# Turning the stored states' rows with VectorE and a scratch instead of TensorE, with the skip term of the stream tokens ahead and the decay moved

## The chip, the cores and the metric

The kernel runs on one core of a Trainium2 chip. Its engines are TensorE (PE in the profile; PEld is its weight load), VectorE (DVE), ScalarE (ACT), GpSimd (POOL) and SyncE (SP). Each works through its own queue in order; semaphores tie the queues together. SP, ACT and POOL issue DMAs. The metric is device microseconds for one execution; less is better. Before the change the median of three runs is 2634.31 us (2633.36 to 2634.69).

## What is computed

One layer of a hybrid encoder, for 256 tokens of a new stream (prompt) and 8 running streams of 16 tokens each, 384 tokens in all. The part that matters here is the state-space branch: per head h, the output of a token t is what the tokens before it in its chunk give, what the stored state gives, and a skip term.

```python
y = jnp.einsum('btsgr,bsgrp->btgrp', cb[..., None] * decay, xdt)
y = y + jnp.einsum('btgn,bgrpn->btgrp', Cc, h) * jnp.exp(cum)[..., None]
h = h * jnp.exp(last)[..., None, None] + jnp.einsum('bsgn,bsgr,bsgrp->bgrpn', Bc, w_end, xdt)
...
y = y + d_skip[..., None] * xh
a_ssd = gated_rmsnorm(y.reshape(b, L, D_INNER), z, ssd_norm)
```

The prompt starts from a zero state, so the second line matters only for the 128 tokens of the running streams. All is float32; the large products split each operand into a rounded high part and the rest (three products each).

## The kernel before

Activations lie with channels on partitions and the 384 tokens along the free axis: 256 prompt tokens, then 128 stream tokens. Most of the time goes into projections: `proj` multiplies 128 output channels' weights with all tokens, in two halves of eight weight tiles. A half's weights come by a DMA on SP (`wfetch`, L63) into one of three buffers and are split by ACT (`wh_...`, L70) and DVE (`wl_...`, L71), each into one of three buffers, so that a split is at most two halves ahead of TensorE. A half takes TensorE 3.9 us (24 products, whose starts are 0.163 us apart).

The state-space stage is a loop over 8 groups g. In each, ten projections run on TensorE: four heads' pairs of channels as tiles x0 to x3, the group's B and C, and four gate tiles z0 to z3. A convolution (`conv_in`, `taps`) follows each x, B and C tile on DVE and ACT. `turned` turns x and B tiles token-major: a DVE transpose of 32x32 blocks, four DMAs on POOL's queue into a scratch `t_scr` that move the blocks to their place, and reads from it.

The four channel tiles of a group make two pairs, `D.p[0]` and `D.p[1]` (four heads each). TensorE does the small products of a pair in one uninterrupted block between projections. The block of pair 0 stands behind z3 of its own group, that of pair 1 behind x2 of the next. It has these parts, by line of the profile:

- `t_pp` (L750): the prompt's new state. In pair 1's block `t_cb` (L695) follows, C times B.
- `t_yT` (L717): two 128x128 transposes of `yis`, the stored state's part of y, scaled by the decay and token-major, to channel-major in the columns 256 to 383 of the PSUM tiles `Y` (one for each of the two channel tiles).
- `t_Y` (L736): 24 products of 64x64 tiles, the part within the chunks, into `Y` and `Yb`. For the stream tokens they add to what the transposes left.
- `t_yi` (L704): C times the stored state `hs`, for the next pair; `yside` (DVE, L790) scales it into `yis`.
- `state` (L865): four tiles `su`, which DVE adds to `hs` (L874).

`Y`, `Yb`, `su` and the norm's `bc_g` come from one pool of six PSUM buffers, `cb` too. Behind the block, `final` on DVE adds skip term and `Y` for all 384 tokens (L889), then `Yb` (L900), and multiplies with z (L901).

`dside` (L856) multiplies the loaded state with its decay, 128x2048 elements in one DVE instruction, after `t_yi` has read it and before `state` adds to it. For pair 0 it stands in the program ahead of z1; `fside` (L850) masks the pair's decay matrix E; `finish` and `store` norm the group before, with a chain of small DVE instructions (L187 to L191). The rest of `pd`'s tiles are SBUF tiles of this stage.

The order on each queue is not the program's order: a scheduler places the instructions, and `behind(...)`, `later()` (behind the latest weight split of ACT and DVE) and `dve_later()` hold some of them back. Behind the stage, during the last eight gate projections (`gate_b`), `aload` reads the branch's 32 normed tiles back from `a_scr` through SP (L1094) and splits them (L1098, L1099).

Of the kernel before, what the change touches and what calls it, by code (L numbers as in the profile page):

```python
# [14 lines left out]
P = 128  # L15
# [6 lines left out]
G = 8  # L22
# [11 lines left out]
def build(ctx, tc, io):  # L34
# [18 lines left out]
    def sstile(name):  # L53
        return pss.tile([P, 512], F32, tag="ss", name=name)
# [19 lines left out]
    def dve_later():  # L74
        return behind(cut[1])
# [138 lines left out]
    ma_scr = [dram.tile([P, T], F32, name=f"ma_scr{i}") for i in range(KD)]  # L214
    gb_scr = [dram.tile([P, T], F32, name=f"gb_scr{i}") for i in range(KD)]
    t_scr = [dram.tile([T, P], F32, name=f"t_scr{i}") for i in range(40)]
    d_scr = dram.tile([P, NH], F32, name="d_scr")
    cum_scr = dram.tile([NH, T], F32, name="cum_scr")
    dec_scr = dram.tile([NH, NB], F32, name="dec_scr")
# [363 lines left out]
    with tc.tile_pool(name="phd", bufs=2, reuse_waits="tile") as pd, tc.tile_pool(  # L583
# [126 lines left out]
                    )  # L710
            return i

        def t_yT(S):
            S.Ys = []
            for q in range(2):
                Y = sstile(f"Y{S.nm}_{q}")
                i = te.transpose(Y[:, TP:T], S.yis[:, q], ident)  # L717
                S.Ys.append(Y)
            S.Yb = sstile(f"Yb{S.nm}")
            return i  # L720

        lower, upper = slice(0, 64), slice(64, P)

        def t_Y(S):
            for q in range(2):
                Ya, Yb = S.Ys[q], S.Yb[:, q * TP : q * TP + TP]
                for r, sb, e0, n, o, c0 in (
                    (lower, 0, 0, TP, Ya, 0),
                    (upper, 0, 64, 192, Yb, 0),
                    (upper, 1, TP, P, Yb, 64),  # L730
                    (lower, 1, TP + 64, 64, Ya, 192),
                    (lower, 2, T + 64, 64, Ya, TP + 64),
                    (upper, 2, T, 64, Yb, 192),
                ):
                    for h in range(2):
                        i = te.matmul(  # L736
                            o[h * 64 : h * 64 + 64, c0 : c0 + n],
                            S.xdt[r, q, sb, h * 64 : h * 64 + 64],
                            S.E[r, q * 2 + h, e0 : e0 + n],
                            start=r is upper and q + sb == 0,  # L740
                            stop=sb > 0,
                            skip_group_check=True,
                        )
            return i
# [43 lines left out]
        def yside(S):  # L788
            S.yis = pd.tile([P, 2, P], F32, tag="yis", name=f"yis{S.nm}", bufs=1)
            S.ready = v.tensor_tensor(  # L790
                S.yis.rearrange("p j (h q) -> p (j h) q", h=2),
                S.yi.rearrange("p (h q) -> p h q", h=4),
                tok[:, 10, S.h0 : S.h0 + 4].unsqueeze(2).to_broadcast([P, 4, 64]),
                ALU.mult,
            )

        def xside(S):
            S.xdt = pd.tile([P, 2, 3, P], F32, tag="xdt", name=f"xdt{S.nm}", bufs=1)
# [59 lines left out]
        def state(S):  # L858
# [18 lines left out]
            lump(t_su)  # L877
            gp.dma_start(io["new_ssm_s"][S.qd], S.hs)

        def final(S):  # L880
            D, g = S.D, S.g
            pe = pd.tile([P, 2, P], F32, tag="pe", name=f"pe{S.nm}", bufs=1)
            s.copy(pe, even_odd(S.pp))
            s.dma_start(io["new_ssm_p"][S.qd], pe.rearrange("p j n -> p (j n)"))
            if S.jp == 0:
                D.ssum = pd.tile([P, T], F32, tag="ssum", name=f"ssum{g}", bufs=1)
            for q, j in enumerate(S.js):
                x, z = D.xs[j], D.zs[j]
                i = v.scalar_tensor_tensor(  # L889
                    out=x,  # L890
                    in0=x,
                    scalar=vec[:, V_DSK + g * 4 + j : V_DSK + g * 4 + j + 1],
                    in1=S.Ys[q][:, :T],
                    op0=ALU.mult,
                    op1=ALU.add,
                )
# [41 lines left out]
        for g in range(G + 1):  # L938
            if g == G:
                S = prev.p[1]  # L940
                work = [
                    [lambda: xside(S)],
                    [lambda: hside(S), lambda: eside(S, 0)],
                    [],
                    [lambda: eside(S, 1)],
                    [lambda: dside(S)],
                    [lambda: expside(S)],
                    [lambda: fside(S, 0), lambda: fside(S, 1)],
                    [],
                ]  # L950
# [9 lines left out]
                lump(lambda: t_yT(prev.p[1]))  # L960
# [46 lines left out]
            if g:  # L1007
                dside(prev.p[1])
                fside(prev.p[1], 0)
            D.CT = conv(u0 + 3, 40 + g, "CT", 2)  # L1010
            D.done = silu[0]
            if g:
                fside(prev.p[1], 1)
            cside(D)
            b2 = conv_in(u0 + 4, g * 4 + 2)
            S = D.p[0]
# [2 lines left out]
                lump(lambda: t_pp(prev.p[1], S.py))  # L1019
            lump(lambda: t_cb(D))  # L1020
            if g:
                lump(lambda: t_yT(prev.p[1]))
                lump(lambda: t_Y(prev.p[1]))
            lump(lambda: t_yi(S))
            mside(D)
# [1 line left out]
            if g:  # L1027
                state(prev.p[1])
                final(prev.p[1])
            D.xs.append(taps(b2, g * 4 + 2, "xs", 6))  # L1030
            with nullcontext() if g else behind(S.ready):
                xside(S)
# [42 lines left out]
            final(S)  # L1075
            if g:
                with behind(S.taken):
                    store(prev)
# [515 lines left out]
```

## Time and profile before

| | us |
|---|---|
| median of three runs | 2634.31 |
| the profiled execution's own time | 2633.2 |
| its span, first to last instruction | 2631.4 |
| TensorE busy in the span | 2621.3 |
| DVE busy in the span | 1573.0 |
| one group of the state-space stage (985.00 to 1072.70) | 87.70 |

The span is what the trace covers. A row of the timeline gives the start from the span's beginning, the length, engine, line, operation, what it writes and reads, the size and, in brackets, how long the engine was idle before and what ended that. A row of the grouped views gives count, busy time and the mean of one in ns. Granted clock is 0.999 of full speed.

### The profile page before, as it was taken

The page shows a single profiled execution, that of the slowest core. Times are in us where ns is not written, and L with a number is a line of the kernel's source. Part 1 is how long each engine was busy: PE and PEld are TensorE (multiplying, and loading weights), DVE is VectorE, ACT ScalarE, POOL GpSimd, SP SyncE. Part 2 cuts the span into 40 slices and gives each one's busy share as a digit, 9 for nine tenths or more (in the row PEclk, how much of TensorE's full clock was granted, in tenths as well). Part 3 has the DMA queues.
Part 4 walks back from the last instruction along what each step waited for, and adds up shares of the span by engine and source line. Part 5 has one row for each costly group of instructions (what it writes and reads, how often), then busy time and mean ns, then how long its engine had stood idle before and what let it go on. Part 6 is the DMA issues. An engine that isn't in the chain of part 4 may idle for free.

```text
span 2631.4 us, 40780 instructions
## 1 busy us (share of the span) xinstructions
PE 2621.3 (100%) x16189; PEld 2523.4 (96%) x16189; DVE 1573.0 (60%) x2286; ACT 1159.7 (44%) x1789; POOL 368.6 (14%) x545
## 2 busy tenths in 40 slices
PE   9999999999999999999999999999999999999998
PEld 9999999999999999999999989999999999989897
DVE  6685335799999999967444436434444444444446
ACT  6443324657565756555333336433333333333233
POOL 0000003245444444411000000000000000000000
PEclk9999999999999999999999999999999999999999
DMA  7445446667676767757545544444444444444443
GB/s 276 150 133 156 148 147 223 201 210 238 224 239 211 235 228 238 233 188 260 165 160 160 195 149 133 144 136 136 134 134 135 136 136 136 136 136 136 135 135 131
DMA packets 134256, 456.33 MB, mean 173 GB/s; under 512 B 20545, under 2 KB 27521, under 8 KB 129073
## 3 DMA queue, kind: packets, MB, share of 16 engines
q1 hardware_dynamic: 103552, 361.44, 43.0%
q0 software_dynamic: 23456, 77.47, 8.5%
q10 hardware_dynamic: 7056, 14.81, 1.8%
q8 instruction: 127, 2.08, 0.3%
q14 instruction: 65, 0.52, 0.1%
HBM read 409.27 MB, written 44.37 MB: 172 GB/s over the span
## 4 chain that ended last, share of the span: by engine, by line
PE 99%; DMA 0%; DVE 0%; ACT 0%; SPq 0%; issue 0%; DVEq 0%
PE pj_up L101 6%; PE pj_up L103 6%; PE pj_up L102 6%; PE wd L156 6%; PE wd L155 6%; PE wd L154 6%; PE pj_x L101 5%; PE pj_x L102 5%; PE pj_x L103 5%; PE pj_sp L102 3%; PE pj_z L103 3%; PE pj_z L102 3%; PE pj_z L101 3%; PE pj_sp L103 3%; PE pj_sp L101 3%; PE pj_gb L101 2%
## 5 line engine op out<-in xcount | busy, mean ns | idle before, releaser
L101 PE MATMUL pj_up<-x1h,wh_up 128*128 128x384 f32 (+1 forms) x1024 | 333.7, 326 | 0.0
L103 PE MATMUL pj_up<-x1h,wl_up 128*128 128x384 f32 (+1 forms) x1024 | 333.4, 326 | 0.0
L102 PE MATMUL pj_up<-x1l,wh_up 128*128 128x384 f32 (+1 forms) x1024 | 333.4, 326 | 0.0
L71 DVE TENSOR_TENSOR wl_wd<-w_wd,wh_wd 128x1024 fp32r<-128x1024 f32 x126 | 154.4, 1225 | 240.3 <-ACT wh_wd L70 240.3
L154 PE MATMUL wd<-wh_wd,hh 128*128 128x512 f32 x756 | 286.5, 379 | 0.0
L155 PE MATMUL wd<-wl_wd,hh 128*128 128x512 f32 x756 | 286.5, 379 | 0.0
L156 PE MATMUL wd<-wh_wd,hl 128*128 128x512 f32 x756 | 286.5, 379 | 0.0
L70 ACT ACTIVATE wh_wd<-w_wd 128x1024 fp32r<-128x1024 f32 x126 | 133.1, 1057 | 321.5 <-PE wd L156 261.0
L70 ACT ACTIVATE wh_up<-w_up 128x1024 fp32r<-128x1024 f32 x126 | 133.1, 1057 | 291.9 <-PE pj_up L102 231.7
L71 DVE TENSOR_TENSOR wl_up<-w_up,wh_up 128x1024 fp32r<-128x1024 f32 x126 | 154.4, 1225 | 178.1 <-ACT wh_up L70 178.0
L101 PE MATMUL pj_x<-xgh,wh_x 128*128 128x384 f32 x768 | 251.9, 328 | 0.0
L102 PE MATMUL pj_x<-xgl,wh_x 128*128 128x384 f32 x768 | 250.4, 326 | 0.0
L103 PE MATMUL pj_x<-xgh,wl_x 128*128 128x384 f32 x768 | 250.4, 326 | 0.0
L102 PEld LDWEIGHTS pj_up<-x1l,wh_up 128*128 128x128 f32 x1024 | 193.6, 189 | 0.2
L101 PEld LDWEIGHTS pj_up<-x1h,wh_up 128*128 128x128 f32 x1024 | 193.6, 189 | 0.2
L103 PEld LDWEIGHTS pj_up<-x1h,wl_up 128*128 128x128 f32 x1024 | 193.6, 189 | 0.0
L101 PE MATMUL pj_z<-xgh,wh_z 128*128 128x384 f32 x512 | 166.9, 326 | 0.0
L102 PE MATMUL pj_z<-xgl,wh_z 128*128 128x384 f32 x512 | 166.9, 326 | 0.0
L103 PE MATMUL pj_z<-xgh,wl_z 128*128 128x384 f32 x512 | 166.9, 326 | 0.0
L101 PE MATMUL pj_sp<-abh,wh_sp 128*128 128x384 f32 x512 | 166.9, 326 | 0.0
L102 PE MATMUL pj_sp<-abl,wh_sp 128*128 128x384 f32 x512 | 166.9, 326 | 0.0
L103 PE MATMUL pj_sp<-abh,wl_sp 128*128 128x384 f32 x512 | 166.9, 326 | 0.0
(351 smaller groups left out, 6373.6 us busy)
## 6 DMA issues: line engine op xcount, KB each, us to landing
w_up<-w_up SPq DMA_DIRECT2D x128, 512.0 KB, 3.5
w_wd<-w_down SPq DMA_DIRECT2D x128, 512.0 KB, 3.5
w_x<-w_in SPq DMA_DIRECT2D x96, 512.0 KB, 3.9
w_z<-w_in SPq DMA_DIRECT2D x64, 512.0 KB, 4.4
w_sp<-w_ssd SPq DMA_DIRECT2D x64, 512.0 KB, 3.5
w_ga<-w_ga SPq DMA_DIRECT2D x32, 512.0 KB, 3.6
w_pp<-w_pp SPq DMA_DIRECT2D x32, 512.0 KB, 3.4
hs<-ssm POOLq DMA_DIRECT2D x16, 1024.0 KB, 6.3
```

The source lines that it names most:

```text
L70: cut[0] = s.activation(h, w, AF.Copy)
L71: cut[1] = v.tensor_tensor(l, w, h.bitcast(F32), ALU.subtract)
L101: te.matmul(out, wh, xh, start=first, stop=False, **how)
L102: te.matmul(out, wh, xl, start=False, stop=False, **how)
L103: return te.matmul(out, wl, xh, start=False, stop=last, **how)
L154: te.matmul(out, mh, vh, start=k == 0 and b != held, stop=False, skip_group_check=b == held)
L155: te.matmul(out, mh, vl, start=False, stop=False, skip_group_check=b == held)
L156: last[0] = te.matmul(out, ml, vh, start=False, stop=k == nk - 1, skip_group_check=b == held)
```

## The change

The transposes `t_yT` go. In their place `yspread` lets DVE transpose the 32x32 blocks of `yis` right after `yside` (128x256), and four DMAs on POOL's queue write them to a new scratch `y_scr`, where they lie channel-major. `yfetch` reads them back into an SBUF tile `yT` with a DMA on ACT's queue, some three projections later. `preside` (two DVE instructions of 128x128) then forms skip term plus `yT` for the stream tokens in x itself, ahead of the block. `final` adds `Y` in two instructions in place of one: skip term and `Y` for the 256 prompt tokens, and `Y` alone for the second half of the stream tokens (64 columns; the first half lies in `Yb`). In `t_Y` the first product into `Y` now starts the accumulation. For pair 0, `dside` moves from ahead of z1 to behind z2 and `preside`.

```diff
+    y_scr = [dram.tile([TP, P], F32, name=f"y_scr{i}") for i in range(2 * G)]
...
-        def t_yT(S):
-            S.Ys = []
-            for q in range(2):
-                Y = sstile(f"Y{S.nm}_{q}")
-                i = te.transpose(Y[:, TP:T], S.yis[:, q], ident)
-                S.Ys.append(Y)
+        def t_Y(S):
+            S.Ys = [sstile(f"Y{S.nm}_{q}") for q in range(2)]
             S.Yb = sstile(f"Yb{S.nm}")
...
-                            start=r is upper and q + sb == 0,
+                            start=sb == 0 and (r is lower or q == 0),
...
+        def yspread(S):
+            S.yb = pd.tile([P, TP], F32, tag="yb", name=f"yb{S.nm}", bufs=1)
+            v.transpose(S.yb, S.yis.rearrange("p j n -> p (j n)"))
+            scr = y_scr[S.qd]
+            for q in range(4):
+                p32 = slice(q * 32, q * 32 + 32)
+                gp.dma_start(
+                    scr[:, p32].rearrange("(j a) b -> a j b", a=32), S.yb[p32].rearrange("p (j b) -> p j b", b=32)
+                )
+
+        def yfetch(S):
+            S.yT = pd.tile([P, 2, P], F32, tag="yT", name=f"yT{S.nm}", bufs=1)
+            with later():
+                s.dma_start(S.yT, y_scr[S.qd].rearrange("(q p) t -> p q t", q=2))
...
+        def preside(S):
+            for q, j in enumerate(S.js):
+                x = S.D.xs[j][:, TP:]
+                with dve_later():
+                    v.scalar_tensor_tensor(
+                        out=x, in0=x, scalar=dskip(S.g, j), in1=S.yT[:, q], op0=ALU.mult, op1=ALU.add
+                    )
...
-                i = v.scalar_tensor_tensor(
-                    out=x,
-                    in0=x,
-                    scalar=vec[:, V_DSK + g * 4 + j : V_DSK + g * 4 + j + 1],
-                    in1=S.Ys[q][:, :T],
-                    op0=ALU.mult,
-                    op1=ALU.add,
-                )
+                xp, xl = x[:, :TP], x[:, TP + 64 :]
+                Y = S.Ys[q]
+                i = v.scalar_tensor_tensor(out=xp, in0=xp, scalar=dskip(g, j), in1=Y[:, :TP], op0=ALU.mult, op1=ALU.add)
+                v.tensor_tensor(xl, xl, Y[:, TP + 64 : T], ALU.add)
...
             with nullcontext() if g else behind(S.split):
                 bside(D)
-            dside(S)
+            yfetch(S)
             zproj(1)
...
             fside(S, 1)
             zproj(2)
+            preside(S)
+            dside(S)
             zproj(3)
             S1 = D.p[1]
             S1.py = mmtile(f"py{S1.nm}")
             lump(lambda: t_pp(S, S1.py))
-            lump(lambda: t_yT(S))
             lump(lambda: t_Y(S))
             lump(lambda: t_yi(S1))
             yside(S1)
             state(S)
             final(S)
+            yspread(S1)
```

For pair 1, `yspread` stands behind `final` of the pair before, `yfetch` ahead of the next group's C tile and `preside` behind `fside`; the last group's pair 1 has the same calls among the gate projections.

What the scheduler makes of it on DVE's queue, group 6, pair 0. Before, the decay (`hs<-hs,decb`) stands between the splits of B and the weights of z2:

```order
L766 TENSOR_TENSOR Bhl_11045<-Bt_10489,Bhl_11045 128x256
L768 SCALAR_TENSOR_TENSOR Bd_11046<-BD_10490,vec,Bd_11046 128x256
L856 TENSOR_TENSOR hs_0_10592<-hs_0_10592,decb 128x2048
L71 TENSOR_TENSOR wl_z_2_0_11056<-w_z_2_0_11053,wh_z_2_0_11055 128x1024
L71 TENSOR_TENSOR wl_z_2_1_11090<-w_z_2_1_11087,wh_z_2_1_11089 128x1024
L850 TENSOR_TENSOR E_0_10944<-E_0_10944,cbm_10802 128x1024 x2
```

The weights of z2 are the next thing that TensorE needs from it. After the change the decay and the two skip terms (`xs<-xs,vec,yT`) stand here, between the weights of z3 and the first read of `Y` by `final`:

```order
L896 SCALAR_TENSOR_TENSOR xs_10521<-xs_10521,vec,yT_0_11193 128x128
L189 TENSOR_TENSOR na_g_11272<-ny_g_11273 128x384
L896 SCALAR_TENSOR_TENSOR xs_10722<-xs_10722,vec,yT_0_11193 128x128
L190 TENSOR_TENSOR na_g_11272<-na_g_11272,ssum_10423 128x384
L865 TENSOR_TENSOR hs_0_10724<-hs_0_10724,decb 128x2048
L191 SCALAR_TENSOR_TENSOR ny_g_11273<-na_g_11272,ny_g_11273 128x384
L1062 TENSOR_TENSOR zs_2_11349<-pj_z_2_11288,rstd 128x384
L71 TENSOR_TENSOR wl_x_0_11359<-w_x_0_11356,wh_x_0_11358 128x1024
L71 TENSOR_TENSOR wl_x_1_11389<-w_x_1_11386,wh_x_1_11388 128x1024
L1062 TENSOR_TENSOR zs_3_11416<-pj_z_3_11355,rstd 128x384
L71 TENSOR_TENSOR wl_x_0_11522<-w_x_0_11519,wh_x_0_11521 128x1024
L911 SCALAR_TENSOR_TENSOR xs_10521<-xs_10521,vec,Y_0_0_11426 128x256
```

So three instructions have come in ahead of the read of `Y`, two of them new, and none has left that stretch. On SP's queue, at the end of the last group, the first four reads of `a_scr` (`ar`) stood between the weights of z3 before:

```order
L63 DMA w_z_3_0_12194<-w_in 128x1024
L1094 DMA ar_13114<-a_scr_72 128x384
L1094 DMA ar_13120<-a_scr_73 128x384
L1094 DMA ar_13156<-a_scr_74 128x384
L1094 DMA ar_13162<-a_scr_75 128x384
L63 DMA w_z_3_1_12224<-w_in 128x1024
```

Now the same four stand among the weights of the last gate projections:

```order
L63 DMA w_gb_1_13480<-w_gb 128x1024
L1114 DMA ar_13290<-a_scr_72 128x384
L1114 DMA ar_13296<-a_scr_73 128x384
L1114 DMA ar_13332<-a_scr_74 128x384
L1114 DMA ar_13338<-a_scr_75 128x384
L63 DMA w_gb_0_13527<-w_gb 128x1024
```

They have moved behind 25 weight loads (the last of z3 and 24 of the gate), and the other 28 follow them in a changed mix with the weights.

More of the change, by code (lines that the diff above doesn't have):

```diff
@@ L711, in t_yi @@
             return i
-        def t_yT(S):
-            S.Ys = []
-            for q in range(2):
-                Y = sstile(f"Y{S.nm}_{q}")
-                i = te.transpose(Y[:, TP:T], S.yis[:, q], ident)
-                S.Ys.append(Y)
-            S.Yb = sstile(f"Yb{S.nm}")
-            return i
         lower, upper = slice(0, 64), slice(64, P)
         def t_Y(S):
+            S.Ys = [sstile(f"Y{S.nm}_{q}") for q in range(2)]
+            S.Yb = sstile(f"Yb{S.nm}")
             for q in range(2):
@@ L878, in state, with dskip @@
             gp.dma_start(io["new_ssm_s"][S.qd], S.hs)
+        def dskip(g, j):
+            return vec[:, V_DSK + g * 4 + j : V_DSK + g * 4 + j + 1]
+        def preside(S):
[5 more added lines that the diff above has]
+                    )
         def final(S):
@@ L944, in build @@
                     [],
-                    [lambda: eside(S, 1)],
+                    [lambda: eside(S, 1), lambda: yfetch(S)],
                     [lambda: dside(S)],
                     [lambda: expside(S)],
-                    [lambda: fside(S, 0), lambda: fside(S, 1)],
+                    [lambda: fside(S, 0), lambda: fside(S, 1), lambda: preside(S)],
                     [],
@@ L959, in build @@
                 py = mmtile("pp_last")
-                lump(lambda: t_yT(prev.p[1]))
                 lump(lambda: t_Y(prev.p[1]))
@@ L1009, in build @@
                 fside(prev.p[1], 0)
+            if g:
+                yfetch(prev.p[1])
             D.CT = conv(u0 + 3, 40 + g, "CT", 2)
@@ L1013, in build @@
                 fside(prev.p[1], 1)
+                preside(prev.p[1])
             cside(D)
@@ L1021, in build @@
             if g:
-                lump(lambda: t_yT(prev.p[1]))
                 lump(lambda: t_Y(prev.p[1]))
@@ L1029, in build @@
                 final(prev.p[1])
+            yspread(S)
             D.xs.append(taps(b2, g * 4 + 2, "xs", 6))
```

## The prediction

> **What bounds the kernel now.** I read the share of busy time and the chain that ended last first.
>
> ```profile
> PE 2621.3 (100%) x16189; PEld 2523.4 (96%) x16189; DVE 1573.0 (60%) x2286; ACT 1159.7 (44%) x1789; POOL 368.6 (14%) x545
> PE 99%; DMA 0%; DVE 0%; ACT 0%; SPq 0%; issue 0%; DVEq 0%
> ```
>
> TensorE is busy for 2621.3 of 2631.4 us, and the chain runs through it alone. Work taken from it is gained in full, as long as nobody makes it wait. So the second view is the stage that the change touches, over one group (one period of the loop over g; columns: PE, PEld, DVE, ACT, POOL busy with counts, clock, DMA share, GB/s).
>
> ```profile
> 985.00:1072.70 87.70, 87.70 (x672) 85.76 (x672) 80.07 (x124) 56.11 (x106) 41.09 (x56) 1.00 0.69 229
> ```
>
> DVE, 60% busy on the page, is 91% busy here (80.07 of 87.70 us). TensorE does not wait in this group, but DVE is close enough that the moment at which each of its results comes decides. The third view is therefore the timeline, TensorE first, at the block of pair 0 of group 6 (columns: start, length, engine, line, operation, count).
>
> ```profile
> 1024.88 0.83 PE L750 MATMUL py<-xhl,Bhl 128*128 128x256 f32 x6
> 1025.55 0.38 PE L717 MATMUL Y<-cst,yis 128*128 128x128 f32 x2
> 1025.86 0.43 PE L736 MATMUL Y<-E,xdt 64*64 64x256 f32 x2
> ...
> 1028.36 0.72 PE L865 MATMUL su<-xd,Bd 32*128 32x256 f32 x16
> ```
>
> The four su tiles and the three Y tiles of a pair share six PSUM buffers, so the fourth su tile takes the buffer of the pair's first Y and cannot start before DVE has read it (L889). Against that, DVE's timeline just before:
>
> ```profile
> 1005.93 2.29 DVE L856 TENSOR_TENSOR hs<-hs,decb 128x2048 f32<-128x2048 f32 x1
> 1008.13 2.35 DVE L71 TENSOR_TENSOR wl_z<-w_z,wh_z 128x1024 fp32r<-128x1024 f32 x2
> ...
> 1025.08 0.56 DVE L1044 TENSOR_TENSOR zs<-pj_z,rstd 128x384 f32<-128x384 f32 x1 [0.99 <-PE pj_z L103]
> 1026.07 1.23 DVE L71 TENSOR_TENSOR wl_x<-w_x,wh_x 128x1024 fp32r<-128x1024 f32 x1 [0.43 <-ACT wh_x L70]
> 1027.21 0.61 DVE L889 SCALAR_TENSOR_TENSOR xs<-xs,vec,Y 128x384 f32<-128x384 f32 x1
> ```
>
> L889 ends at 1027.82, su begins at 1028.36: a margin of 0.54 us, with 1.42 us (0.99 + 0.43) of DVE idle time ahead of it.
>
> **The transposes removed.** Their own row, and what they take of the path:
>
> ```profile
> L717 PE MATMUL Y<-cst,yis x32: 272/273/273, 499.6 to 1148.1; 128*128 128x128 f32 x32
> ```
>
> Two of them stand in each of 16 blocks. From the first one's start to the next product 0.31 us pass (1025.55 to 1025.86). The two together last 0.38 and one 0.273, so the second starts 0.11 after the first; the other 0.20 is one more 0.11 and some 0.09 of the passage from whole-array work to 64*64 tiles, which a product that now follows L750 directly will pay too. Gain per block 0.22 us, at most 0.31; over 16 blocks 3.5 us, at most 5.0. I take 3.5, because the passage stays. The start flag moves from the transpose to the first Y product and adds no instruction: nothing, unless a started accumulation is slower, of which no row says anything.
>
> The Trainium skill, "VectorE: DVE Perf Modes", section "Rules for kernel authors", speaks against the change: a 128x128 transpose belongs on TensorE where PSUM will do as its target. Its section "The three transpose paths" has 390 ns for TensorE and 311 ns for VectorE (bf16). By 390 ns each, 32 would give back 12.5 us, an estimate from that page; here one lasts 273 ns and follows the one before it after 0.11 us, so the trace does not agree, and the sum goes by the trace.
>
> **What DVE gets for it.** These rows give the prices; the new forms themselves are not in the trace, forms of the same size are:
>
> ```profile
> L645 DVE STREAM_TRANSPOSE xb<-xs 128x384 f32<-128x384 f32 x35 | 20.1, 574 | 9.5 <-ACT xs L626 9.5
> L421 DVE SCALAR_TENSOR_TENSOR d<-win,pbuf 128x256 f32<-128x256 f32 x16 | 6.8, 425 | 0.3
> L424 DVE SCALAR_TENSOR_TENSOR d<-win,pbuf 128x128 f32<-128x128 f32 x16 | 4.6, 286 | 0.0
> L391 DVE TENSOR_TENSOR pbuf<-pj_p,rstd 128x64 f32<-128x64 f32 x16 | 3.5, 216 | 0.0
> ```
>
> Independent DVE instructions overlap by some 0.085 us (2.29 long, next start 2.20 later). A pair gains one 128x256 transpose (between 0.29, half of L645 and a bit, and 0.57, all of it; by two thirds of its length and the overlap, 0.33), two skip terms (2 x 0.20) and, for each of two channel tiles, a 128x256 and a 128x64 read (0.34 + 0.13) in place of L889's 0.52, which saves 0.05 each. Sum 0.63 us a pair, 1.3 a group: DVE goes from 80.1 to 81.4 of 87.7 us. Its amount is hidden under TensorE. Four more DMA issues a pair put 8 x 0.6 = 5 us a group on POOL's queue, 41.1 busy of 87.7, so that is hidden too.
>
> ```profile
> t_scr<-xb POOLq DMA_DIRECT2D x160, 48.0 KB, 4.2
> xT<-t_scr POOLq DMA_DIRECT2D x96, 64.0 KB, 3.4
> ```
>
> The detour through the scratch costs about 4 x 0.6 + 4.2 + 3.4 = 10 us by these rows of a like detour. A pair's scaled rows exist about half a group (44 us) before the skip term uses them; even 15 us of queueing on POOL leaves cover. If the cover were gone, DVE would stand at the skip term with the weight splits behind it.
>
> **The decay moved, which I think decides.** It leaves the place ahead of two wl_z splits and stands, with the two skip terms, ahead of three more splits and L889. Added just ahead of pair 0's block: 2.20 + 0.40 = 2.60 us. Taken off: the 1.42 us of idle time, and whatever DVE is early by. That is less than the 2.20 taken away, since the second split after the old place waits for its weights anyway:
>
> ```profile
> 1007.37 1.06 ACT L70 ACTIVATE wh_z<-w_z 128x1024 fp32r<-128x1024 f32 x1 [1.99 <-DMA w_z<-w_in]
> 1009.87 1.06 ACT L70 ACTIVATE wh_z<-w_z 128x1024 fp32r<-128x1024 f32 x1 [1.45 <-DMA w_z<-w_in]
> 1015.11 1.06 ACT L70 ACTIVATE wh_z<-w_z 128x1024 fp32r<-128x1024 f32 x1 [1.33 <-DMA w_z<-w_in]
> ```
>
> The first of these ends at 1008.43; its split starts at 1009.26 now (half of 2.35 after 1008.13) and can start 0.83 earlier, not 2.20. So DVE reaches L889 2.60 - 1.42 - 0.83 = 0.35 us later. TensorE comes 0.44 earlier (two blocks without transposes since DVE last waited for it). The shorter read gives 0.05 back. 0.35 + 0.44 - 0.05 = 0.74 against a margin of 0.54: su waits 0.2 us. Lower bound 0 (the idle time may take more), if the loads land as now. They may not:
>
> ```profile
> w_up<-w_up SPq DMA_DIRECT2D x128, 512.0 KB, 3.5
> w_z<-w_in SPq DMA_DIRECT2D x64, 512.0 KB, 4.4
> ```
>
> The same load is 0.9 us slower in this stage than in a quiet one. The change puts 128 KB written and 128 KB read for each pair into it, and moves POOL's other transfers, the 1 MB state loads and stores among them, up to 2.5 us later, towards these three loads. Once DVE stands waiting for them, a late landing comes through one to one. Bounds: nothing, and as much again on two loads in a row, 1.8 us; I take 0.8, nearer the lower one since the added bytes are few beside the loads'. So 1.0 us a block, 8.0 over eight groups; bounds 0 and 16.
>
> **Pair 1's block.** The same buffer rule:
>
> ```profile
> 1070.81 0.86 DVE L786 TENSOR_TENSOR cbm<-cb,cst 64x256 f32<-64x256 f32 x2
> 1071.70 0.61 DVE L889 SCALAR_TENSOR_TENSOR xs<-xs,vec,Y 128x384 f32<-128x384 f32 x1
> 1072.46 0.72 PE L865 MATMUL su<-xd,Bd 32*128 32x256 f32 x16
> ```
>
> L889 ends at 1072.31, margin 0.15; TensorE comes 0.22 earlier, the read is 0.05 shorter: 0.02 us, with the 0.31 gain instead 0.11. I take 0.1 in eight blocks, 0.8 us, bounds 0 and 2.
>
> **The branch reads on SP.** Four reads of a_scr that stood in the last group now stand among the last gate weights, where the queue alternates between both, in order:
>
> ```profile
> 1217.43 0.81 SPq L1094 DMA_DIRECT2D ar<-a_scr  x2
> 1219.50 0.33 SPq L63 DMA_DIRECT2D w_gb<-w_gb  x1
> 1219.97 1.07 SPq L1094 DMA_DIRECT2D ar<-a_scr  x2
> 1215.71 1.23 DVE L71 TENSOR_TENSOR wl_gb<-w_gb,wh_gb 128x1024 fp32r<-128x1024 f32 x1 [0.39 <-ACT wh_gb L70]
> 1218.64 0.33 PE L103 MATMUL pj_gb<-xgh,wl_gb 128*128 128x384 f32 x1
> ```
>
> Two pairs of them cost 0.8 to 1.1 us each of the queue; the margin of the split is 1.70 (1216.94 to 1218.64). I take 1.0 us of wait, bounds 0 and 2.5, once.
>
> **Sum.** -3.5 + 8.0 + 0.8 + 1.0 = +6.3 us on the profiled execution's 2633.2 (span 2631.4 and 1.8 around it): 2639.5. The median of the three runs is 1.1 higher, 2634.3, so 2640.6 there.
>
> **Rivals.** First, the decay is covered and nothing new waits: -5.0 to -3.5 from the transposes, up to +1 for the reads, 2630.3. For it: 1.42 us of idle time and 0.83 of earlier start nearly pay for 2.60. Against it: the 0.54 us of margin is already spoken for by the 0.44 that TensorE gains. Second, on the far side, the loads themselves become the wait: with POOL's transfers in their way the z weights land so late that the splits, not the Y read, hold TensorE. It decides from about 2 us later landing, since 0.83 + 1.42 are all that DVE has in hand; at 2 us a group, 16 - 3.5 + 2 gives 2649. For it: three loads in a row already hold ScalarE for 1.3 to 2.0 us. Against it: no load holds TensorE today. Third, a transpose costs the path its whole 273 ns: 8.7 us gained against 9.8 lost, 2635.4. For it there is only the length in its row, against it the starts 0.11 apart. A full-length transpose is also what the section "The three transpose paths" of the Trainium skill's page "VectorE: DVE Perf Modes" would charge.
>
> **How the numbers follow.** Chances: forecast 0.58, first rival 0.24, second 0.13, third 0.05. A measurement of this kernel can tell 0.2% (5.3 us) from no change. Faster than that needs more than the 5.0 us that the transposes hold at most: 0.04, out of the first rival. The rest of that (0.20), the third (0.05) and the lower part of the forecast (0.12: a wait of under 0.9 us a block) make 0.37 for no change; slower has 0.59. Range from all waits at their lower bound with 0.31 gained per block (-5.0, 2629) to twice the forecast's wait with the tail (8 x 2 + 2.5 + 0.8 - 3.5 = +15.8, 2650). The forecast alone: 2636 to 2650.
>
> **What would show it.** In the profile of the changed kernel: no transpose in the blocks, and 0.2 us from the last L750 product to the first Y product; DVE idle for 1 to 2.5 us ahead of a wl_z split for lack of weights, where the decay was, and busy without a gap from the decay to the Y read; su starts spread apart, 0.5 to 1.5 us between its third and fourth tile in pair 0's block; little of it in pair 1's. The prediction is wrong if pair 0's su still starts all four tiles at once, if a wait for the scratch's rows appears on DVE or ScalarE, or if a weight split holds TensorE.

## The result and the profile after

| | before | changed |
|---|---|---|
| median of eleven runs, us | 2634.0 | 2640.18 |
| lowest and highest | 2633.36, 2634.69 | 2638.34, 2644.12 |
| span of the profiled execution | 2631.4 | 2639.6 |

The ratio is 1.0025, with a 95% interval from 1.0016 to 1.0034: slower by 6.2 us. 2640.6 was forecast. That the total fits does not say that its terms do. They are taken apart here, and two of them turn out wrong by some 4 and 3 us with opposite signs, a third by 2.

First the share of busy time and the chain that ended last, of the changed kernel:

```profile
PE 2624.7 (99%) x16157; PEld 2524.4 (96%) x16157; DVE 1582.4 (60%) x2366; ACT 1161.7 (44%) x1789; POOL 362.9 (14%) x609
...
PE 83%; DVE 8%; ACT 3%; DMA 2%; issue 2%; POOL 1%; DVEq 0%; ACTq 0%; SPq 0%; POOLq 0%
```

Before, the chain ran through TensorE for 99%. Now it leaves TensorE at each of its waits and runs a long way back through DVE, ScalarE and loads until it meets TensorE again. So 17% of the chain is elsewhere, although the kernel lost 0.3%. A chain's shares say who stands behind the waits, not how long they are.

How long, the waits of TensorE tell (waited for, us in total, times, longest), with the matching stretch of six groups from one pair 1 block to another, first before, then changed (length; PE, PEld, DVE, ACT, POOL busy; clock; DMA share; GB/s):

```profile
PE su L874 <- DVE xs L912: 3.2, 5, 1.2
PE pj_z L103 <- DVE wl_z L71: 1.5, 7, 0.2
...
PE pj_gb L103 <- DVE wl_gb L71: 0.5, 1, 0.5
```

```profile
542.14:1068.11 525.97, 525.97 (x3986) 514.33 (x3985) 479.97 (x738) 335.93 (x630) 243.43 (x333) 1.00 0.69 228
```

```profile
542.44:1074.41 531.97, 528.04 (x3962) 513.83 (x3961) 486.34 (x797) 336.40 (x629) 236.34 (x384) 1.00 0.70 231
```

A group takes 88.66 us in place of 87.66. DVE has gained 6.4 us over six groups, 1.06 a group. There are three kinds of wait: su on the read of `Y`, a z product on a weight split, and one gate product. The second kind was forecast not to be there.

The sums of this view are too small. It takes the modelled end of the product ahead as the start of the wait. The timeline shows that at z1's third product of group 6 (TensorE alone; starts and lengths):

```profile
1005.35 0.33 PE L101 MATMUL pj_z<-xgh,wh_z 128*128 128x384 f32 x1
1005.52 0.33 PE L102 MATMUL pj_z<-xgl,wh_z 128*128 128x384 f32 x1
1006.05 0.43 PE L103 MATMUL pj_z<-xgh,wl_z 128*128 128x384 f32 x1 [0.21 <-DVE wl_z L71]
1006.32 0.33 PE L101 MATMUL pj_z<-xgh,wh_z 128*128 128x384 f32 x1
```

The products' starts stand 0.16 apart in the stream. Here they are 0.53 and 0.27 apart, which is 0.37 + 0.11 lost where the bracket says 0.21. So all waits below are worked out from starts, against the same places of the kernel before. Over the profiled executions:

| place | us, changed minus before |
|---|---|
| ahead of the stage (its first product starts at 419.34 in place of 418.81) | +0.5 |
| 32 transposes, 16 blocks | -3.5 |
| su waits in pair 0's blocks | +3.8 |
| su waits in pair 1's blocks, last block | +2.7, +0.3 |
| ahead of z1 (groups 1 to 7) | +3.4 |
| head of pair 0's block of group 6 | +0.3 |
| gate projections behind the last block | +0.7 |
| sum | +8.2 |

The spans differ by 8.2 too. The first row arises in the kernel's first 15 us, ahead of everything that the diff touches; the executions of the other kernels differ from that of the kernel before by -0.4 to +1.4 there. Everything behind the stage, 1377.19 us from the first `sp` product to the last of `wd`, is the same to the hundredth.

### The profile page after: what moved, and what is told of

Same layout as the page of the kernel before. It is cut to its first block, busy times and chain, and to the rows that moved or that the text cites. A ratio compares the mean times of both kernels' runs of the same rounds, so it can differ in the third digit from the quotient of the medians.

```text
span 2639.6 us, 40973 instructions
## 1 busy us (share of the span) xinstructions
PE 2624.7 (99%) x16157; PEld 2524.4 (96%) x16157; DVE 1582.4 (60%) x2366; ACT 1161.7 (44%) x1789; POOL 362.9 (14%) x609
## 4 chain that ended last, share of the span: by engine, by line
PE 83%; DVE 8%; ACT 3%; DMA 2%; issue 2%; POOL 1%; DVEq 0%; ACTq 0%; SPq 0%; POOLq 0%
PE pj_up L103 6%; PE pj_up L101 6%; PE pj_up L102 6%; PE wd L156 6%; PE wd L155 6%; PE wd L154 6%; PE pj_sp L103 3%; PE pj_sp L102 3%; PE pj_sp L101 3%; PE pj_z L103 2%; PE pj_z L101 2%; PE pj_z L102 2%; PE pj_x L101 2%; PE pj_ga L101 2%; PE pj_pp L103 2%
```

## The experiments

All waits are those of the one profiled execution of each kernel; the times are medians. The profiled execution can lie some us beside the median, which is said where it matters.

**The decay put back.** Only this differs from the changed kernel, on DVE too:

```diff
             yfetch(S)
+            dside(S)
             zproj(1)
...
             preside(S)
-            dside(S)
             zproj(3)
```

> The changed kernel with the decay of pair 0 back at its old place ahead of z1; all else stays as changed. In the profiled execution of the changed kernel the fourth su tile of pair 0's blocks waits 3.9 us in all, in four of eight groups. Theory (the decay stands between late z weights and the read of Y): these waits go to under 0.5 us in all, the split of z2's first half keeps about 0.4 us of its 2.58 us of slack, and the time falls by 3.9 us, from 2640.2 to about 2636.3. Rival (the added scratch traffic makes the z weights land late, wherever the decay stands): pair 0's waits stay above 2 us in all and the time stays above 2638. In both, the 0.47 us a group ahead of z1's first split and the waits in pair 1's blocks (3.0 us in all) stay.

2636.24 us, ratio 1.0008 (1.0000 to 1.0017), 3.9 us less than the change. Pair 0's blocks wait 0.1 us in all, the wait ahead of z1 stays at 0.45 to 0.48 a group, pair 1's blocks wait 1.4. Its waits of TensorE in the two kinds:

```profile
PE pj_z L103 <- DVE wl_z L71: 1.4, 7, 0.2
...
PE su L874 <- DVE xs L912: 0.3, 1, 0.3
```

The decay's place makes pair 0's waits; the scratch traffic is still there and makes none.

**The decay alone.** The kernel before, with `dside(S)` moved from ahead of `zproj(1)` to behind `zproj(2)`.

> The kernel before with the decay of pair 0 moved behind z2 and nothing else changed. By the sum of the prediction the read of Y comes 2.20 - 1.42 - 0.83 = -0.05 us later, so nothing waits when the loads land as before, and where one of the z weights lands late up to 1 us a group comes through: 2634 to 2637, some su waits in pair 0's blocks, none in pair 1's and none ahead of z1's first split. Rival (the move alone makes pair 0's waits): 2634.0 + 3.9 = 2638. Second rival (the decay hurts nothing at its new place, the skip terms do): 2634.0 and no wait.

2635.34 us, ratio 1.0005 (0.9996 to 1.0014). Around the decay the scheduler also places some steps of the norm in another order here. Five of eight pair 0 blocks wait for nothing, two wait 0.14 and 0.15, and the last group's waits 1.7, with 0.5 more ahead of its z projections. Pair 1's wait nothing. So the move alone is nearly free, as reckoned, until one load is late: it takes away the cover, and the 0.52 us of skip terms and TensorE's earlier arrival then use it up.

**Pair 1 without its skip terms.** The calls `preside(prev.p[1])` and that of the last group taken out.

> The changed kernel without the two skip terms of pair 1: y of these channels lacks the skip and the stored states' part for the stream tokens. Theory (pair 1's su waits for the read of Y because these two instructions, 0.52 us, stand on DVE ahead of a chain DVE, ScalarE, DVE whose idle time cannot absorb them): the 3.0 us of waits in pair 1's blocks fall to under 0.5 us, and the wait ahead of z1's first split falls by 0.2 of its 0.47 us a group, since DVE comes out of the block earlier: 2640.2 less 3.0 and less 1.4, about 2636. Rival (DVE's idle time ahead of that read, 1.2 us, absorbs the two instructions as it was taken to, and the waits come from the earlier arrival of TensorE alone): pair 1's waits stay near 3 us, 2640.

2640.0 us, ratio 1.0022 (1.0013 to 1.0031): the time does not move. Pair 1's waits fall from 2.7 to 1.6, but five of seven stay at 0.17 or 0.18 each, and the wait at z1 does not move (0.45 to 0.48). In this execution pair 0's waits were 4.9 and ate the rest. Both theories were partly wrong. A floor of 0.17 a block comes from TensorE's earlier arrival: `no_transposes`, below, adds no skip term and no transpose on DVE and has the same 0.17 in six of these seven blocks. The skip terms add to it in some groups only.

The margin of 0.15 us that the prediction saw there was none. Wherever su waits in the changed kernel, its fourth product starts 0.15 us behind the end of the read (in the timeline of pair 0's block below: 1034.55 to 1034.70), so 0.15 is what the hand-over takes. In all seven pair 1 blocks of the kernel before, su stood just that far behind the read (1072.31 to 1072.46 in the prediction's lines). TensorE comes 0.22 earlier, and 0.17 of it is lost again.

**No scratch traffic.** The writes to `y_scr` and the read from it left out, the skip terms read a constant:

```diff
-                gp.dma_start(
-                    scr[:, p32].rearrange("(j a) b -> a j b", a=32), S.yb[p32].rearrange("p (j b) -> p j b", b=32)
-                )
...
-                s.dma_start(S.yT, y_scr[S.qd].rearrange("(q p) t -> p q t", q=2))
+            S.yT = cst[:, :TP].rearrange("p (q t) -> p q t", q=2)
```

> The changed kernel without the writes to the new scratch and the reads from it: the skip terms add a constant tile in place of the stored states' part, which y then lacks. DVE's transposes and skip terms stay. Theory (order on DVE and ScalarE sets the waits, traffic a part of pair 0's alone): 0.47 us a group ahead of z1's first split and 3.0 us in pair 1's blocks stay; pair 0's waits fall from 3.9 to about 1.6 (0.2 a group), 2638. Rival (contention of the scratch traffic makes all of pair 0's waits): they go to 0, 2636.3. Second rival (the traffic does nothing): 2640.

2642.54 us, ratio 1.0031 (1.0018 to 1.0043), not faster. Pair 0's waits were 1.9, as expected, but pair 1's 4.2, and behind one of these blocks the x products lost another 1.7 at half the granted clock (the last section). The traffic delays the z loads somewhat (the table below), and taking it away brings no time.

**What pair 0 waits for.** In the changed kernel and in the two above that keep its decay and its turning in place, one number fixes the wait: when ScalarE starts to split z2's second half, counted from the group's first z0 product. Groups 1 to 7, start and su wait of pair 0's block in us:

| kernel | 1 | 2 | 3 | 4 | 5 | 6 | 7 |
|---|---|---|---|---|---|---|---|
| changed | 15.32, 1.15 | 14.00, 0 | 14.33, 0.15 | 15.11, 0.93 | 13.90, 0 | 16.03, 1.57 | 13.97, 0 |
| no_skip_pair1 | 15.72, 1.55 | 14.88, 0.73 | 14.77, 0.58 | 15.22, 1.05 | 14.02, 0 | 14.62, 0.47 | 14.64, 0.46 |
| no_traffic | 14.32, 0.17 | 14.81, 0.66 | 12.32, 0 | 15.25, 1.10 | 13.89, 0 | 14.05, 0 | 13.64, 0 |
| before | 14.27, 0 | 13.52, 0 | 14.68, 0 | 14.62, 0 | 14.77, 0 | 14.01, 0 | 15.28, 0 |

The wait is the start less 14.2, one to one. (Group 6 of the changed kernel lost 0.3 of it at the head of the block, whose first product starts at 1029.72, as soon as DVE has read z2's products; that read stands behind the decay too.) The kernel before has starts as late and waits for none, because its decay does not stand behind them. Their mean is 14.45 before, 14.67 changed and 14.04 without the traffic: the loads come 0.2 us later, not 0.8. With the starts of the kernel before, the rule would give 2.6 us over the seven groups, an estimate, so most of the 3.8 needs no later load. In `decay_alone` the wait is the start less 15.0 (starts 15.14, 15.14 and 17.27): the 0.8 between the two is what skip terms and TensorE's earlier arrival use up. The chain of waits of the changed kernel runs through this split in group 6 (start, length, what):

```profile
1004.78 1.23 DVE wl_z L71
1006.02 7.45 DMA w_z<-w_in
1013.58 1.07 ACT wh_z L70
1014.67 0.87 DVE wl_z L71
```

The first row is z1's first split, the one that TensorE waited for at 1006.05. It frees the buffer into which the load of z2's second half goes; the load ends late, and the splits follow at once. On DVE's timeline the rest of the way to su, and the block on TensorE:

```profile
1014.67 1.23 DVE L71 TENSOR_TENSOR wl_z<-w_z,wh_z 128x1024 fp32r<-128x1024 f32 x1 [2.97 <-ACT wh_z L70]
...
1026.45 2.28 DVE L865 TENSOR_TENSOR hs<-hs,decb 128x2048 f32<-128x2048 f32 x1
...
1031.21 1.23 DVE L71 TENSOR_TENSOR wl_x<-w_x,wh_x 128x1024 fp32r<-128x1024 f32 x1 [0.41 <-ACT wh_x L70]
1032.35 0.55 DVE L1062 TENSOR_TENSOR zs<-pj_z,rstd 128x384 f32<-128x384 f32 x1
1032.82 1.22 DVE L71 TENSOR_TENSOR wl_x<-w_x,wh_x 128x1024 fp32r<-128x1024 f32 x1
1033.95 0.48 DVE L911 SCALAR_TENSOR_TENSOR xs<-xs,vec,Y 128x256 f32<-128x256 f32 x1
1034.34 0.21 DVE L912 TENSOR_TENSOR xs<-xs,Y 128x64 f32<-128x64 f32 x1
```

```profile
1033.09 0.38 PE L874 MATMUL su<-xd,Bd 32*128 32x256 f32 x3
1034.70 0.68 PE L874 MATMUL su<-xd,Bd 32*128 32x256 f32 x13 [1.23 <-DVE xs L912]
```

DVE stands idle for 2.97 us where the decay was, for lack of weights, and is then all but busy until the read of `Y`. Three su products run, and the fourth, the first of the tile that takes `Y`'s buffer, waits for it.

**Where the wait at z1 comes from: later turning, and the transposes alone.** `turn_late` moves `yspread(S)` behind the scaling of the x rows. `turn_late_back` puts it behind z0, the read ahead of z2 and the decay back. The edit of `turn_late`:

```diff
                 final(prev.p[1])
-            yspread(S)
...
             with nullcontext() if g else behind(D.done):
                 eside(S, 0)
+            yspread(S)
```

> The changed kernel with pair 0's turning of yis (the DVE transpose and the four writes) one place later in the program, behind the scaling of the pair's x rows and E; nothing else is edited. The scheduler then puts the split of z1's first half ahead of the convolution's steps on DVE instead of behind them. Theory (the 0.47 us a group ahead of z1's first split comes from this order, and the late split holds back the buffer that w_z of z2's second half is loaded into, which lands later and so makes part of pair 0's waits): the wait ahead of z1 goes to 0 (3.3 us), that load is issued about 0.8 us earlier, pair 0's waits fall from 3.8 to about 2; 2640.2 less 5, about 2635. Rival (the amount of DVE work makes the wait: the 0.36 us of the transpose still stand ahead of that split): 0.3 to 0.47 us a group stay, 2639 to 2640.

> The changed kernel with the decay of pair 0 back at its old place, pair 0's turning moved behind the latest z split after z0, and its read from the scratch moved ahead of z2. If the waits add up as taken apart, only those remain that come from TensorE's own earlier arrival: 0.17 us in each of seven pair 1 blocks and 0.28 in the last, 1.5 us in all against 3.5 gained: about 2 us under the kernel before, 2632. Rival (later reading makes a new wait for the rows at the skip terms, or the decay at its old place now makes the split of z2's first half late): 2635 or more.

2658.31 us (ratio 1.0093, 1.0079 to 1.0107) and 2656.33 us (1.0088, 1.0074 to 1.0102): far off, on the wrong side of both theories. The wait at z1 is gone in both, but 2.2 us or more are lost ahead of it, at z0's second half, in seven and in six groups. `no_transposes` is the kernel before without its transposes; `Y` is read as in the change:

```diff
-            lump(lambda: t_yT(S))
             lump(lambda: t_Y(S))
...
+                i = v.scalar_tensor_tensor(out=xp, in0=xp, scalar=dsk, in1=Y[:, :TP], op0=ALU.mult, op1=ALU.add)
+                v.tensor_tensor(xl, xl, Y[:, TP + 64 : T], ALU.add)
```

> The kernel before with the 32 transposes taken out and nothing in their place: y lacks the stored states' part, and the skip term for the stream tokens, since Y is read as in the change (256 and 64 columns). The decay stays at its old place. Theory (two transposes take 0.22 us of a block's path): 3.5 us gained, of which the read of Y in pair 1's blocks gives back 7 x 0.17 and the last block 0.28, since its margin was 0.15: about 2.0 us under the kernel before, 2632. Rival (a transpose takes its whole 273 ns): 8.7 us gained, 2626 to 2627.

2652.46 us, ratio 1.0074 (1.0061 to 1.0086). Less work on the engine that bounds the kernel, and 18.8 us slower. Its own blocks gained what was forecast (2.50 us from the first `Y` product to su, where it was 2.81, and 0.09 more ahead of it), but 2.2 to 4.6 us are lost in each group ahead of z1. In four of the seven groups 1.7 of that is lost behind the wait, at half the granted clock (the last section), 6.7 us in all. ScalarE's timeline in group 3 and the two products that wait show why:

```profile
736.29 1.28 ACT L838 ACT_TABLE_LOAD   x1
737.58 1.93 ACT L838 ACTIVATE E<-E 128x2048 f32<-128x2048 f32 x1
739.53 1.28 ACT L626 ACT_TABLE_LOAD   x1
740.82 0.62 ACT L626 ACTIVATE xs<-cacc,vec 128x384 f32<-128x384 f32 x1
...
742.38 1.04 ACT L70 ACTIVATE wh_z<-w_z 128x1024 fp32r<-128x1024 f32 x1
```

```profile
743.48 0.43 PE L101 MATMUL pj_z<-xgh,wh_z 128*128 128x384 f32 x1 [1.02 <-ACT wh_z L70]
744.74 0.43 PE L103 MATMUL pj_z<-xgh,wl_z 128*128 128x384 f32 x1 [0.67 <-DVE wl_z L71]
```

The exponential of E with its two table loads, 4.5 us, stands ahead of the split of z0's second half, and so it does in both turn kernels (group 6 of `turn_late`: exponential at 1009.85, split at 1014.65). Before, the split comes first; in the changed kernel it comes first too, but the silu of x2 has slid from 3.7 us ahead of the split to right ahead of it, since DVE's convolution steps now stand behind the four additions to `hs`. ScalarE's rows, before and changed, group 6:

```profile
988.38 0.61 ACT L626 ACTIVATE xs<-cacc,vec 128x384 f32<-128x384 f32 x1
...
992.07 1.04 ACT L70 ACTIVATE wh_z<-w_z 128x1024 fp32r<-128x1024 f32 x1
...
995.46 1.91 ACT L845 ACTIVATE E<-E 128x2048 f32<-128x2048 f32 x1
```

```profile
996.83 0.62 ACT L627 ACTIVATE xs<-cacc,vec 128x384 f32<-128x384 f32 x1 [0.69 <-DVE cacc L623]
997.35 1.04 ACT L70 ACTIVATE wh_z<-w_z 128x1024 fp32r<-128x1024 f32 x1
...
1000.85 1.91 ACT L854 ACTIVATE E<-E 128x2048 f32<-128x2048 f32 x1
```

Group 6 runs 4.2 us later in the changed kernel, so its exponential comes 1.2 us late, and the split of z1's first half behind it 0.8 late, where it had 0.5 us to spare. No line of the diff touches these instructions. Three orders of one stretch, all chosen by the scheduler after an edit somewhere else.

**The order held.** Three kernels fix that stretch by hand. `held` is the changed kernel with

```diff
                 xside(S)
-                hside(S)
...
             xturned(D, g, 3)
+            with later() if g else behind(S.ready):
+                hside(S)
...
             zproj(0)
+            with dve_later():
+                yspread(S)
...
-                expside(S)
+            with behind(S.split):
+                expside(S)
```

(and `yfetch` ahead of z2). `held_mid` has `yspread` where `turn_late` has it, ahead of z0's second split on DVE, and `yfetch` where the change has it. `held_back` is `held` with the decay at its old place.

> The changed kernel with the order behind pair 1's block held near that of the kernel before (the splits of the x rows behind the latest weight split, the exponential of E behind the split of the x rows) and pair 0's turning behind z1's splits; the decay stays at its new place. Theory: the 0.47 us a group ahead of z1's first split is order and DVE work in this stretch, so it goes to under 0.1 us (3.3 us); w_z of z2's second half, which waits for the buffer that z1's first split frees, is issued some 0.7 us earlier in its group, and pair 0's waits fall from 3.8 to about 2: 2640.2 less 5, about 2635. Rival: the order has no part in pair 0's waits, they stay near 3.8, 2637.

> As held, but pair 0's turning stands on DVE ahead of z0's second split; the two orders differ on DVE in this one instruction (0.36 us). It parts order from amount. If the amount counts, the wait ahead of z1's first split comes back by up to 0.36 us a group (at most 2.5 us in all, 2636 to 2638) and the load of z2's second half is issued that much later; if only the order counted, it stays under 0.1 and the time is that of held.

> As held, with the decay of pair 0 at its old place. If the waits add up as taken apart, only those remain that TensorE's earlier arrival makes: 0.17 us in seven pair 1 blocks and 0.28 in the last, 1.5 us against 3.5 gained: 2632, some 2 us under the kernel before. Rival (the decay at its old place, ahead of z2's first split, now makes that split late, or the later reading of the scratch makes a wait at the skip terms): 2634 or more.

| kernel | us | ratio, interval | wait at z1, seven groups |
|---|---|---|---|
| held | 2637.9 | 1.0013, 1.0005 to 1.0022 | 0 |
| held_mid | 2635.87 | 1.0006, 0.9997 to 1.0015 | 0 |
| held_back | 2633.08 | 0.9997, 0.9988 to 1.0006 | 0 |

The wait at z1 that came in every group is gone in all three, with the transpose ahead of the split too: it was the order, not the 0.36 us. In `held` the load of z2's second half is issued 1.3 us earlier in its group, yet pair 0's waits stay (4.6 us): the load then takes 6.8 us in place of 6.1, and the turning has moved into the stretch ahead of the read of `Y`. The rival's reading holds there. Putting the decay back is worth 4.8 us on top.

The other two profiled executions were the slowest of their eleven (2641.17 and 2635.6), and their losses stand elsewhere. `held_mid` waits 4.7 us in pair 0's blocks and 4.4 in pair 1's, and at the head of one pair 0 block its first product waits, as above, for a read of z products that stands behind the decay; `held_back` waits for nothing in pair 0's blocks, but 3.6 in pair 1's. One row of each:

```profile
PE py L744 <- DVE zs L1063: 0.6, 1, 0.6
```

```profile
PE su L874 <- DVE cbm L780: 1.0, 1, 1.0
```

The second is group 2's block, 2.0 us by the starts. It stands behind a load of x's weights for which ScalarE was idle for 1.90 us at 695.94; from there the chain that ended last runs through ScalarE and DVE to su.

**The change again, and the two repairs together.** `held_mid_back` is `held_mid` with the decay put back.

> The changed kernel itself, once more, beside the runs of the others: about 2640, with the same kinds of waits (0.47 us ahead of z1's first split in seven groups; pair 0's blocks some 0.5 us on average, uneven by group; pair 1's 0.17 or more in each).

> The changed kernel with the order behind pair 1's block held, the turning ahead of z0's second split and the decay of pair 0 back at its old place. With the turning out of the stretch between z1's splits and the read of Y, pair 0's and z1's waits are both gone; 1.5 us of waits from TensorE's earlier arrival stay against 3.5 gained: 2632, and 2632 to 2633 by held_back, which it differs from by one instruction's place. Rival (the transpose ahead of z0's second split brings the wait at z1 back): 2634 to 2636.

The change came to 2641.39 us, ratio 1.0029 (1.0019 to 1.0039), with 3.2 us in seven groups ahead of z1, 5.1 in pair 0's blocks, 3.8 in pair 1's and nothing in the gate stage. `held_mid_back` came to 2633.84, ratio 1.0000 (0.9991 to 1.0009), 2.0 us less than `held_mid`. Its profiled execution shows the sum as taken apart, first by the page's span and its chain, then by the only row of su in the waits of TensorE (another 1.2 us went ahead of the first block, 0.9 of it at the start of the stage):

```profile
span 2630.9 us, 40958 instructions
...
PE 98%; DMA 1%; issue 0%; DVE 0%; ACT 0%; SPq 0%; DVEq 0%; POOLq 0%; ACTq 0%
```

```profile
PE su L874 <- DVE xs L912: 0.3, 1, 0.3
```

Nothing in pair 0's blocks, nothing ahead of z1, 0.17 to 0.23 in each of pair 1's, 0.3 in the last block. No version beats the kernel before by more than its measurement tells: what is gained on TensorE, 3.5 us, leaves 2 us after pair 1's floor, and the medians show 0.9 of it in `held_back` and none in `held_mid_back`.

## Why the prediction was right, and where it was not

- **Transposes, -3.5.** Right: 0.22 us in each of the 16 blocks, -3.5. The passage from whole-array work to 64*64 tiles (0.09) stayed, as taken. The rival with 273 ns each has fallen in every kernel without transposes.
- **DVE's added work, hidden.** The amount was about right: 1.06 us a group, forecast 1.3, of which the new forms are these:

```profile
L793 DVE STREAM_TRANSPOSE yb<-yis 128x256 f32<-128x256 f32 x16 | 7.0, 440 | 0.0
L896 DVE SCALAR_TENSOR_TENSOR xs<-xs,vec,yT 128x128 f32<-128x128 f32 x32 | 10.3, 345 | 0.0
L912 DVE TENSOR_TENSOR xs<-xs,Y 128x64 f32<-128x64 f32 x32 | 6.9, 214 | 0.0
```

  The detour through the scratch made no wait at the skip terms, also as taken. What failed is "Its amount is hidden under TensorE" as the whole answer. The stretch behind pair 1's block was not compared in the two orders at all, and there the order had changed. Price: +3.4 us ahead of z1, forecast nothing. That "a weight split holds TensorE" was named as what would make the prediction wrong, and it does, though not by the second rival's mechanism: those weights had landed long before, and the split stood behind other work.
- **The decay, +8.0.** The mechanism was right, and is shown by putting it back, which takes pair 0's waits to 0.1 us or nothing in all three kernels where it was done (3.9, 4.8 and 2.0 us less by the medians), and by moving it alone. The term was mis-sized: 3.8 us in one execution, 5.1 in another. The margin of 0.54 held 0.15 of hand-over. It was priced as 0.2 of arithmetic and 0.8 of later landing in every group. The loads came only 0.2 later; what counts is that they scatter from 13.9 to 16.0, and the part above 14.2 comes through. Three or four of eight groups pay 0.9 to 1.6, the others nothing or little. So the first sign of being wrong, su starting all four tiles at once, is there too, in four groups of eight.
- **Pair 1's blocks, +0.8.** Too low: 2.7 and 3.8 in seven blocks, 0.3 in the last. The step that failed is the margin: the 0.15 was the hand-over, so that nearly all of the 0.22 that TensorE gains comes back as a wait of 0.17. What DVE is late by beyond that was not in the sum. With the decay back pair 1 waits 1.4 in `decay_back` and 1.3 in `held_mid_back`, but 3.6 in `held_back`, so that it goes with the decay's place is not shown, and how it is handed from one block to the next was not settled.
- **Branch reads, +1.0.** Right in size where it comes: 0.7 in one execution of the change, 0.7 in `no_traffic`, 1.1 in `no_skip_pair1`, nothing in the second execution of the change. The mechanism is that ScalarE's queue holds the weight split behind the split of a read that lands late:

```profile
1223.98 0.52 ACT L1118 ACTIVATE abh<-ar 128x384 fp32r<-128x384 f32 x1 [1.72 <-DMA ar<-a_scr]
1224.41 1.04 ACT L70 ACTIVATE wh_gb<-w_gb 128x1024 fp32r<-128x1024 f32 x1
```

  With the same order of loads and reads on SP, `decay_back` and `turn_late` lost nothing here, so it seems to be a matter of how the reads land.
- **The sum.** +6.3 was forecast and +6.2 measured by the medians, +8.2 by the profiled executions. That is luck: pair 0's term was some 4 us too high, the missing term at z1 is 3.4, and pair 1's was 2 too low. The direction rests in part on the mechanism that was named, for without the decay's waits the change is still 2.1 us slower (`decay_back`, 2636.24 against 2634.14, a ratio whose interval reaches down to 1.0000); that part comes mostly from z1 (3.3 us there), which was not foreseen.

The rule of the Trainium skill that spoke against the change ("VectorE: DVE Perf Modes", section "Rules for kernel authors": a 128x128 transpose on TensorE where PSUM will do as its target) gives the right side for the change as it was made, but not by its price: the transposes returned 3.5 us, and waits took 11 back. With order and place repaired (`held_mid_back`) no difference either way is left to measure. The Trainium skill, "Perfetto Trace Analysis", section "Optimization Strategy", takes a gap that repeats on the engine that should be full as a possible shortage of buffers. The trace agrees at su, where a seventh tile goes into six; the 0.48 us that repeat at z1 come from an order instead.

## What to carry to other kernels

When a scheduler places the instructions, an edit changes orders that it does not touch: compare the order on every queue of the stage, not only at the edited places, before pricing the edit. Taking work off the bounding engine can cost more than adding some, 18.8 us here. Idle time ahead of an instruction is cover only if nothing late ends it: read over all periods when the load that ends it comes, and let what lies above the threshold through one to one. A margin from the end of one engine's instruction to the start of another's holds the hand-over, 0.15 us here, and only the rest can be used.

## What was unexpected of the hardware

- A wait on TensorE costs more than its bracket: after the late product the next starts 0.27 us later in place of 0.16 (1006.05 to 1006.32), and the wait of 0.21 by the view is 0.48 by the starts.
- A wait on TensorE can cost a second time. In `held_back`, 1.6 us after the late su of group 2's pair 1 block had resumed (722.95), the granted clock fell to 0.50 for 3.41 us (third column from the end), and the x products started 0.32 us apart in place of 0.16: 1.7 us lost.

```profile
724.54:727.95 3.41, 3.41 (x13) 3.41 (x12) 3.41 (x8) 3.14 (x10) 1.35 (x1) 0.50 0.20 72
```

  The same came once in `no_traffic`, twice in each of the two turn kernels and four times in `no_transposes`, and in no other kernel between its first and last 11 us. In other groups of these kernels the same wait of 2.2 us passed without it; what decides this is not shown.
- Issuing a load earlier gained less than that: z2's second half, issued 1.3 us earlier in `held`, landed 0.6 us earlier on average.
- In one step the chain of waits of the changed kernel names the write to the new scratch as what ScalarE waited for ahead of z0's second split:

```profile
995.16 2.18 DMA y_scr<-yb
997.35 0.79 ACT wh_z L70
```

  ScalarE was busy with the silu until then (996.83 and 0.52 until the next start), and without the write (`no_traffic`) the wait behind it is the same 0.45 us a group. An event that ends close to a start need not be its cause.
